# Encoder trunk on one core: residuals go into layer 1's projections and the sample's second SwiGLU without their norm, and the row scale is applied to what comes out

## The chip, the cores and the metric

The kernel runs on one core of a Trainium2 chip. The metric is device microseconds of one execution. Engines are named as in the profile: PE (TensorE, matmuls), DVE (VectorE), ACT (ScalarE), POOL (GpSimd), and SP, which issues nearly all DMAs.

## The reference

Two layers run over a prompt of 1024 tokens and a sample of 512, width 1024, with the same weights. Layer 0 mixes tokens with a Fourier transform, layer 1 with attention; each is followed by a SwiGLU.

```python
def rms_norm(x, g):
    y = xf * lax.rsqrt(jnp.mean(xf * xf, axis=-1, keepdims=True) + EPS)
    return y * g
# layer 1: 8 query heads, 2 key/value heads of 128
h = rms_norm(x, g); q, k, v = split(h @ w_qkv)
q = rope(rms_norm(q, q_gain)); k = rope(rms_norm(k, k_gain))
x = x + softmax(q k^T * 128**-0.5) v @ w_o
# after each layer, inner width 2816
h = rms_norm(x, g)
x = x + (silu(h @ w_gate) * (h @ w_up)) @ w_down
```

The norm's factor is one number a token (a row of x), so it can be taken through a product with weights: `(r*x*g) @ w = r * ((x*g) @ w)`. Queries and keys are normalised once more, head by head.

## The kernel before

Tokens stand in three blocks of 512: block 0 is the sample, 1 and 2 the prompt. A residual is kept transposed, eight tiles of 128 features by 512 tokens. Every fp32 product is made of three matmuls: each operand is split into a rounded part (on ACT, line 242 or 245) and a rest (on DVE or POOL, line 243 or 246), and `mm3` (lines 249 to 251) adds three of the four part products. Three such matmuls are called a triple here.

The code is written as generators, whose `yield` gives an estimated cost; `weave` takes from two of them in turn, the stream F and the stream X, so that their work lies mixed, and a scheduler in the tile framework then sets each engine's order. F and X have PSUM banks and SBUF buffers of their own. The stages: the sample's Fourier mixer; its first SwiGLU with the prompt's mixer (to about 530 us); the prompt's SwiGLU of layer 0 for both blocks at once (`ffn_pair`, to about 1210); then `main_1` in F (the sample's projections, attention, out-projection and second SwiGLU) with `aux_2` in X (the same for the prompt; its reload for the second pair is `moving`); last the prompt's SwiGLU of layer 1, again `ffn_pair`.

- `normed` makes the operand `h` of a projection. From the sums of squares come the factors a token (`rstd`, by `rstd_cols`: four matmuls with a column of ones and a root in small DVE steps); `in_rows` spreads them over the partitions with four matmuls on ones; each of eight residual tiles is multiplied by them on DVE (line 369) into PSUM and split from there (lines 245, 246).
- `normed` is called by `qkv` for the three blocks and by `prepare` for the sample's second SwiGLU. Block 0 is read from DRAM (`xres`), blocks 1 and 2 from SBUF, where `ffn_pair` left them (`kept`).
- `qkv` runs 12 projections of 8 triples. Of each query head the sums of squares go to `ssq`, and one root at the end serves all heads; a key head has a root and rows of its own; a value head is turned on PE and copied out (line 1260).
- `ffn` makes, for each of 22 slices, gate in 8 triples and up in 8, `silu` on ACT (line 851), the product and its split, and the down product into accumulators (line 782). In the sample's first SwiGLU (`here`) it has the row factor applied to gate's and up's sums on DVE (lines 849, 850).
- `attend` takes 128 queries at a time: scores, softmax (`p`), PE transposes of `p` into `pt` (`turned`), and `values` for two such steps.
- `ffn_pair` makes seven products for eight, both for gate and up (tiles `a` of two banks) and for down: `product(k, d, f0)`, 28 for each pair of slices, one triple each, into `chain[d]`, and DVE adds the bank to an accumulator (line 1054). In all pairs of slices but the last the four chains are banks of `bank()` and `bankg()` (tiles `c` and `g`); in the last they are halves of two-bank tiles `a`. Each group of four products reads one operand; the fourth group reads the operand `N4`, kept in the tile `ring`, and it comes from the last gate and up step.

Of the kernel before, what the change touches and what calls it, by code (L numbers as in the profile page):

```python
# [10 lines left out]
F32 = mybir.dt.float32  # L11
# [3 lines left out]
ALU = mybir.AluOpType  # L15
# [110 lines left out]
def trunk_kernel(ctx: ExitStack, tc: tile.TileContext, t: dict):  # L126
# [177 lines left out]
    def rstd_cols(y, sq, n):  # L304

        c = bank()
        for j in range(4):
            pe.matmul(c[:, j : j + 1], sq[:, j * P : (j + 1) * P], ones[:, 0:1], start=True, stop=True)
        rsqrt(y, c[:, 0:4], 1.0 / n, c[:, 8:24])

# [43 lines left out]

    def normed(b, gain, got, ab, held=None):

        settled(b)
        yield 2.0
        r = in_rows(rstd[b])
        h = h_tile(ab)  # L360
        yield 1.0
        for dp in range(NC // 2):
            for dc, ps in zip((2 * dp, 2 * dp + 1), sides()):
                if held is None:
                    x = tmp()
                    sp.dma_start(x, xres[b][:, dc, :])
                else:
                    x = held[dc]
                dve.tensor_tensor(ps, r, x, op=ALU.mult)
                split(h[:, 0, dc], h[:, 1, dc], ps, gain=gain[:, dc : dc + 1])  # L370
            yield 1.5
        got["h"] = h
# [371 lines left out]
    def linear_residual(src, u, b, prev):  # L744

        for n in range(NC):
            w = weights(src[n])
            x = tmp()
            sp.dma_start(x, prev[:, n, :])
            ps = bank()  # L750
            project(w, u, ps)
            dve.tensor_tensor(x, ps, x, op=ALU.add)
            new_residual(b, n, x)
            yield 5.5


    kept, pend = {}, []

    def ffn(layer, b, h, out=None):
        h = h()  # L760
        here = b in resident
        acc = resident.pop(b) if here else accumulators()
# [3 lines left out]
        def halves(ms, wds, f0, dc):  # L766

            box = []

            def half(i):  # L770
                w = wds[dc // 4].rearrange("p h (f c) n -> p h f c n", f=2)
                mm3(box[0], w[:, 0, i, dc % 4], w[:, 1, i, dc % 4], ms[i][:, 0], ms[i][:, 1], i == 0, i == 1)

            def begin():
                box.append(bank())
                if f0 == 0 and not here:
                    sp.dma_start(acc[dc], xres[b][:, dc, :])
                half(0)

            def end():  # L780
                half(1)
                dve.tensor_tensor(acc[dc], box[0], acc[dc], op=ALU.add)  # L782
                if f0 + 2 == NF:
                    new_residual(b, dc, acc[dc], None if out is None else out[:, dc, :])

            return begin, end
# [25 lines left out]
        for fc in range(NF):  # L812
# [19 lines left out]
            for dc in range(NC):  # L832
                if not odd_ and dc == 3:
                    want("gate", fc + 1)
                if fc == NF - 1 and dc == 4:
                    want("B", f0)
                if dc == (2 if odd_ else 4):
                    want("up", fc + 1)
                if not (here and fc == 0):
                    part(wu, h, up, dc)  # L840
                if not odd_:
                    one(2 if dc in (2, 4, 6) else 1)
                elif dc >= 6:
                    one()
                if dc % 2:
                    yield (3.4 if dc > 1 else 2.7) if not odd_ else 2.7 if dc == 7 else 1.36
            s = tmp()
            if here:
                dve.tensor_tensor(ga, ga, first["r"], op=ALU.mult)
                dve.tensor_tensor(up, up, first["r"], op=ALU.mult)  # L850
# [71 lines left out]
    def ffn_pair(layer, blocks, ring, places, outs):  # L922
# [111 lines left out]
        def product(k, d, f0):  # L1034
# [11 lines left out]
            if fresh and f0 + 2 < NF:  # L1046
# [178 lines left out]
    def qkv(b, held=None):  # L1225
        got = {}
        yield from normed(b, g_mix1, got, "ABB"[b], held)
        h = got["h"]
# [13 lines left out]
        def key_sums(j, sq, a):  # L1242

            y = cols.tile([P, 4], F32, tag="yk", name=nm("yk"))
            rstd_cols(y, sq, HD)
# [8 lines left out]
        def turned_values(j, v):  # L1254
# [5 lines left out]
            dve.tensor_copy(vs, vt)  # L1260
            sp.dma_start(dv[b][j - NH - NKV].rearrange("p c n -> p (c n)"), vs)

        def settle():

            now, owed[:] = owed[:], []
            for v in reversed(now):
                v()
# [31 lines left out]
        y = col(4 * NH)  # L1299
        rsqrt(y, ssq.rearrange("p c h -> p (c h)"), 1.0 / HD, bank()[:, 0 : 16 * NH])  # L1300
        dst = slice(4 * b, 4 * b + 4)
# [3 lines left out]
    def attend(blocks, straight, slot):  # L1305
# [6 lines left out]
        for g in range(NKV):  # L1312
# [15 lines left out]
            for h in range(g * GROUP, (g + 1) * GROUP):  # L1328
# [52 lines left out]
                last = None  # L1381
                for qc in range(nk + 1):
                    p = scores(qc) if qc < nk else None
                    yield 0.7 * nb
                    if qc:
                        turned(qc - 1, last)
                        yield 0.8 * nb
                        if qc % 2 == 0:
                            values(qc // 2 - 1)
                            yield 0.8 * nb  # L1390
                    last = p
# [16 lines left out]

    FFN_US, PAIR_US, CHAIN_US, PROMPT_US = 352.0, 678.0, 223.0, 630.0
# [63 lines left out]
    def prepare(b, layer):  # L1473

        yield from normed(b, g_ffn[layer], nxt, "A")
# [65 lines left out]
    def main_1():  # L1541
        yield from qkv(0)
        yield from attend((0,), 0, "A")
        yield from out_projection(0, "A")
# [3 lines left out]
    def aux_2():  # L1548
        for b in (2, 1):
            settled(b)  # L1550
            yield 2.0
# [123 lines left out]
```

## Time and profile before

| | us |
|---|---|
| median of 3 runs (2968.76 to 2973.36) | 2969.23 |
| the profiled execution | 2965.4 |
| its span, first to last instruction | 2963.6 |
| PE busy | 2855.9 |
| DVE busy | 1713.3 |
| POOL busy | 1517.6 |
| ACT busy | 1304.9 |

A row of a group gives line, engine, operation, tiles as out<-in, shapes and the count, then busy time and the mean of one in ns, then the idle time of the engine before it and what ended that. A row of the timeline gives start, length, engine, line and tiles, and in brackets the wait before it with its releaser. A window gives, for PE, weight loads, DVE, ACT and POOL, busy time and number of instructions, then the granted share of PE's clock, the DMA engines' busy share and GB/s. PE's matmuls are pipelined: at full clock, triples of 512 columns start every 0.68 us although each matmul is shown as 0.39 long.

### The profile page before, as it was taken

How to read it: one execution, taken by the hardware profiler on the slowest of the kernel's cores; microseconds unless marked ns; L12 is line 12 of the kernel's file. 1: busy time of each engine (PE TensorE's matmuls, PEld its weight loads, DVE VectorE, ACT ScalarE, POOL GpSimd, SP SyncE). 2: the span in 40 equal slices, each digit the busy share in tenths (PEclk: the TensorE clock that was granted, in tenths of full speed). 3: DMA queues.
4: the chain of work that ended last, by engine and by line, in shares of the span. 5: the costliest groups of instructions: out<-in, count | busy, mean ns of one | idle time of the engine just before them, and what ended most of it. 6: DMA issues, size and time to landing. Idle time of an engine off the chain costs nothing. (4 is left out here: it accounts for less than half of the span.)

```text
span 2963.6 us, 37198 instructions
## 1 busy us (share of the span) xinstructions
PE 2855.9 (96%) x13656; PEld 2350.0 (79%) x13656; DVE 1713.3 (58%) x3031; ACT 1304.9 (44%) x2131; POOL 1517.6 (51%) x932
## 2 busy tenths in 40 slices
PE   7999999999999999998998999999998999999998
PEld 6778878788888887786777888878886788888886
DVE  6674553566666667737646555552244466666666
ACT  5543232333333333646756776663333333333332
POOL 4344264766776774522241122224535767766763
PEclk8999999999999999999999999999999999999999
DMA  7435374766556553632242121115447865565552
GB/s 227 143 116 183 131 270 167 291 218 222 192 186 219 199 175 130 213 93 85 83 150 89 59 91 54 54 57 192 151 168 278 309 235 200 176 219 201 192 195 89
DMA packets 182326, 496.82 MB, mean 168 GB/s; under 512 B 19872, under 2 KB 30112, under 8 KB 180736
## 3 DMA queue, kind: packets, MB, share of 16 engines
q1 hardware_dynamic: 181216, 489.65, 48.5%
q0 software_dynamic: 640, 3.74, 0.4%
q8 instruction: 108, 1.77, 0.2%
q10 hardware_dynamic: 288, 1.05, 0.1%
q14 instruction: 74, 0.61, 0.1%
HBM read 426.21 MB, written 68.16 MB: 167 GB/s over the span
## 5 line engine op out<-in xcount | busy, mean ns | idle before, releaser
L288 POOL TENSOR_TENSOR w<-raw,w 128x1024 fp32r<-128x1024 f32 x200 | 479.0, 2402 | 843.9 <-ACT w L287 832.7
L243 POOL TENSOR_TENSOR w<-raw,w 128x512 fp32r<-128x512 f32 (+1 forms) x464 | 608.3, 1331 | 451.2 <-ACT w L242 445.0
L242 ACT CAST w<-raw 128x512 fp32r<-128x512 f32 (+1 forms) x464 | 279.6, 632 | 538.3 <-PE a L251 173.2
L287 ACT CAST w<-raw 128x1024 fp32r<-128x1024 f32 x200 | 208.7, 1049 | 269.5 <-PE g L251 77.9
L249 PE MATMUL g<-h,w 128*128 128x512 f32 x704 | 279.3, 397 | 9.9 <-ACT w L287 3.4
L251 PE MATMUL g<-h,w 128*128 128x512 f32 x704 | 277.8, 395 | 2.2 <-POOL w L288 2.2
L249 PE MATMUL a<-ring,w 128*128 128x512 f32 x712 | 279.5, 392 | 0.1
L251 PE MATMUL a<-ring,w 128*128 128x512 f32 x712 | 277.5, 390 | 0.0
L250 PE MATMUL a<-ring,w 128*128 128x512 f32 x712 | 277.3, 389 | 0.0
L250 PE MATMUL g<-h,w 128*128 128x512 f32 x704 | 276.8, 393 | 0.0
L1054 DVE TENSOR_TENSOR acc<-g,acc 128x512 f32<-128x512 f32 x280 | 192.5, 687 | 106.9 <-PE g L251 106.6
L1054 DVE TENSOR_TENSOR acc<-c,acc 128x512 f32<-128x512 f32 x280 | 192.4, 687 | 93.7 <-PE c L251 92.1
L249 PE MATMUL c<-mid,w 128*128 128x512 f32 x592 | 232.4, 393 | 13.3 <-ACT mid L242 7.6
L250 PE MATMUL c<-mid,w 128*128 128x512 f32 x592 | 232.6, 393 | 1.2 <-DVE mid L243 1.1
L251 PE MATMUL c<-mid,w 128*128 128x512 f32 x592 | 232.5, 393 | 1.3 <-POOL w L288 1.3
L249 PE MATMUL c<-h,w 128*128 128x512 f32 x480 | 191.5, 400 | 4.3 <-ACT h L245 3.3
L782 DVE TENSOR_TENSOR acc<-c,acc 128x512 f32<-128x512 f32 x176 | 120.9, 688 | 129.2 <-PE c L251 126.5
L250 PE MATMUL c<-h,w 128*128 128x512 f32 x480 | 189.1, 395 | 1.2 <-DVE h L246 0.9
L251 PE MATMUL c<-h,w 128*128 128x512 f32 x480 | 188.9, 394 | 0.0
L249 PEld LDWEIGHTS g<-h,w 128*128 128x128 f32 x704 | 133.0, 189 | 37.1 <-ACT w L287 3.8
L249 PEld LDWEIGHTS a<-ring,w 128*128 128x128 f32 x712 | 133.8, 188 | 33.8 <-DVE mid L243 4.4
L251 PEld LDWEIGHTS g<-h,w 128*128 128x128 f32 x704 | 132.9, 189 | 30.0 <-POOL w L288 3.3
(392 smaller groups left out, 6718.5 us busy)
## 6 DMA issues: line engine op xcount, KB each, us to landing
ring<-mov_B SPq DMA_DIRECT2D x248, 512.0 KB, 5.5
ring<-mov_T SPq DMA_DIRECT2D x88, 512.0 KB, 5.1
raw<-in_gate_dram SPq DMA_DIRECT2D x44, 512.0 KB, 3.6
raw<-in_up_dram SPq DMA_DIRECT2D x44, 512.0 KB, 3.5
raw<-in_down_dram SPq DMA_DIRECT2D x88, 256.0 KB, 3.1
raw<-in_gate_dram SPq DMA_DIRECT2D x88, 256.0 KB, 5.0
raw<-in_up_dram SPq DMA_DIRECT2D x88, 256.0 KB, 5.4
raw<-in_down_dram SPq DMA_DIRECT2D x44, 512.0 KB, 4.1
```

The source lines that it names most:

```text
L242: keep(act.copy(hi, src))
L243: keep(eng.tensor_tensor(lo, src, hi.bitcast(F32), op=ALU.subtract))
L249: pe.matmul(out, lh, rh, start=first, stop=False, **kw)
L250: pe.matmul(out, lh, rl, start=False, stop=False, **kw)
L251: pe.matmul(out, ll, rh, start=False, stop=last, **kw)
L287: pinned(act.copy(flat[:, 0], raw)) if early else act.copy(flat[:, 0], raw)
L288: pool.tensor_tensor(flat[:, 1], raw, flat[:, 0].bitcast(F32), op=ALU.subtract)
L782: dve.tensor_tensor(acc[dc], box[0], acc[dc], op=ALU.add)
L1054: dve.tensor_tensor(acc, chain[d], acc, op=ALU.add)
```

## The change

`normed` is gone. `qkv` and `prepare` split the residual times the gain as it is. In `qkv` the row factor is applied twice to each head's sums of squares and once to the root (`outer`, `by_head`: with sums S of the unscaled head, the factor wanted is r / sqrt(r*r*S/128 + eps)), and to the value copies, which now are four of 128 columns with a factor a partition. The sums of squares of a block are closed (`settled`) at the first head instead of before the operand. In the sample's second SwiGLU the factor is applied to gate's and up's sums, as in the first; its accumulators are taken before the out-projection, which adds into them directly (`staying`), so that the residual is not written to DRAM and read back. Beside this, `ffn_pair` of layer 1 uses the banks `c` and `g` for its last chains too, and the estimated costs in `qkv`, `attend` and `prepare` are others; with `LAG = 1` `attend` issues its steps in the order it had.

```diff
+    def rstd_cols(y, sq, n, outer=None):
...
+        if outer is not None:
+            for _ in range(2):
+                dve.tensor_tensor(c[:, 0:4], c[:, 0:4], outer, op=ALU.mult)
         rsqrt(y, c[:, 0:4], 1.0 / n, c[:, 8:24])
+        if outer is not None:
+            dve.tensor_tensor(y, y, outer, op=ALU.mult)
...
-    def normed(b, gain, got, ab, held=None):
-        settled(b)
-        yield 2.0
-        r = in_rows(rstd[b])
...
-                dve.tensor_tensor(ps, r, x, op=ALU.mult)
-                split(h[:, 0, dc], h[:, 1, dc], ps, gain=gain[:, dc : dc + 1])
...
# linear_residual
-            x = tmp()
+            x = staying[b][n] if b in staying else tmp()
...
-            new_residual(b, n, x)
+            new_residual(b, n, x, stays=b in staying, later=(tl("ss", [TB], F32, "ssF") if n == 0 else ss[b]) if b in staying else None)
...
# ffn
-                if f0 == 0 and not here:
-                    sp.dma_start(acc[dc], xres[b][:, dc, :])
...
+                if fc == 0 and not here and dc == 1:
+                    settled(b)
...
-            if here:
-                dve.tensor_tensor(ga, ga, first["r"], op=ALU.mult)
-                dve.tensor_tensor(up, up, first["r"], op=ALU.mult)
+            if fc == 0 and not here:
+                first["r"] = tl("ss", [TB], F32, "ssF")
+                act.copy(first["r"], in_rows(rstd[b]))
+            dve.tensor_tensor(ga, ga, first["r"], op=ALU.mult)
+            dve.tensor_tensor(up, up, first["r"], op=ALU.mult)
...
# product, in ffn_pair
-            if fresh and f0 + 2 < NF:
+            if fresh and (f0 + 2 < NF or outs is not None):
                 chain[d] = bank() if d % 2 else bankg()
...
# qkv
+        h = h_tile("ABB"[b])
+        yield 0.5
+        for dc in (4, 5, 6, 7, 0, 1, 2, 3):
...
+            split(h[:, 0, dc], h[:, 1, dc], x, gain=g_mix1[:, dc : dc + 1])
+            yield 0.7
...
-            rstd_cols(y, sq, HD)
+            rstd_cols(y, sq, HD, rstd[b])
...
-            dve.tensor_copy(vs, vt)
+            for i in range(4):
+                dve.tensor_scalar(vs[:, i * P : (i + 1) * P], vt[:, i * P : (i + 1) * P], rstd[b][:, i : i + 1], None, op0=ALU.mult)
...
+        by_head = rstd[b].unsqueeze(2).to_broadcast([P, 4, NH])
+        for _ in range(2):
+            dve.tensor_tensor(ssq, ssq, by_head, op=ALU.mult)
...
# attend
+                for qc in range(nk + LAG):
+                    if qc < nk:
+                        ps.append(scores(qc))
+                        yield 0.7 * nb
+                    n = qc - LAG
+                    if n >= 0:
+                        turned(n, ps[n])
+                        yield (0.2 if n % 2 else 2.0) * nb
+                        if n % 2:
+                            values(n // 2)
+                            yield 0.2 * nb
...
# prepare
-        yield from normed(b, g_ffn[layer], nxt, "A")
+        h = h_tile("A")
+        for dc in range(NC):
+            split(h[:, 0, dc], h[:, 1, dc], staying[b][dc], gain=g_ffn[layer][:, dc : dc + 1])
+        nxt["h"] = h
+        yield 1.0
...
# main_1
         yield from attend((0,), 0, "A")
+        staying[0] = accumulators()
         yield from out_projection(0, "A")
...
# aux_2
-        for b in (2, 1):
-            settled(b)
-            yield 2.0
```

What it does to the order is shown at three places. Line numbers of the changed program are its own (its 1366 is 1364 above, 1042 is 1054, 1124 is 1136, 1072 is 1084). First PE at the end of the program, the first four down products of the last pair of slices; before:

```order
L249 MATMUL a_23742<-mid_18667,w_23618 128x512
L250 MATMUL a_23742<-mid_18667,w_23618 128x512
L251 MATMUL a_23742<-mid_18667,w_23618 128x512
L249 MATMUL a_23742<-mid_18667,w_23618 128x512
L250 MATMUL a_23742<-mid_18667,w_23618 128x512
L251 MATMUL a_23742<-mid_18667,w_23618 128x512
L249 MATMUL a_23742<-mid_18669,w_23618 128x512
L250 MATMUL a_23742<-mid_18669,w_23618 128x512
L251 MATMUL a_23742<-mid_18669,w_23618 128x512
L249 MATMUL a_23742<-mid_18669,w_23618 128x512
L250 MATMUL a_23742<-mid_18669,w_23618 128x512
L251 MATMUL a_23742<-mid_18669,w_23618 128x512
```

All four write one tile of two banks. Now, after two products that stand ahead of the last gate step:

```order
L249 MATMUL g_23708<-mid_18637,w_23574 128x512
L250 MATMUL g_23708<-mid_18637,w_23574 128x512
L251 MATMUL g_23708<-mid_18637,w_23574 128x512
L249 MATMUL c_23713<-mid_18637,w_23574 128x512
L250 MATMUL c_23713<-mid_18637,w_23574 128x512
L251 MATMUL c_23713<-mid_18637,w_23574 128x512
L249 MATMUL g_23698<-mid_18639,w_23574 128x512
L250 MATMUL g_23698<-mid_18639,w_23574 128x512
L251 MATMUL g_23698<-mid_18639,w_23574 128x512
L249 MATMUL c_23703<-mid_18639,w_23574 128x512
L250 MATMUL c_23703<-mid_18639,w_23574 128x512
L251 MATMUL c_23703<-mid_18639,w_23574 128x512
```

Each writes a tile of its own, and a tile comes again after four products.

Second PE where the sample's out-projection (`c<-h`) ends, mixed with prompt attention (`a<-w` scores, `c<-ident,p` transposes, `c<-pt` values); before, with the sums of squares (`ss`) behind it:

```order
L249 MATMUL c_13204<-h_10881,w_13199 128x512
L250 MATMUL c_13204<-h_10881,w_13199 128x512
L251 MATMUL c_13204<-h_10881,w_13199 128x512
L249 MATMUL a_13253<-w_12614,w_13178 128x512
L250 MATMUL a_13253<-w_12614,w_13178 128x512
L251 MATMUL a_13253<-w_12614,w_13178 128x512
L249 MATMUL a_13253<-w_12614,w_13178 128x512
L250 MATMUL a_13253<-w_12614,w_13178 128x512
L251 MATMUL a_13253<-w_12614,w_13178 128x512
L1364 MATMUL c_13271<-ident,p_13193 128x128 x4
L1364 MATMUL c_13278<-ident,p_13193 128x128 x4
L308 MATMUL c_13235<-ones,ss_12494 128x1 x4
```

And now, from the transposes that follow the out-projection's last triples:

```order
L1366 MATMUL c_13123<-ident,p_13067 128x128 x4
L1366 MATMUL c_13130<-ident,p_13067 128x128 x4
L251 MATMUL a_13171<-w_12613,w_13168 128x512
L249 MATMUL a_13171<-w_12613,w_13168 128x512
L250 MATMUL a_13171<-w_12613,w_13168 128x512
L251 MATMUL a_13171<-w_12613,w_13168 128x512
L249 MATMUL g_13246<-h_13219,w_13238 128x512
L250 MATMUL g_13246<-h_13219,w_13238 128x512
L251 MATMUL g_13246<-h_13219,w_13238 128x512
L249 MATMUL g_13246<-h_13219,w_13238 128x512
L250 MATMUL g_13246<-h_13219,w_13238 128x512
L251 MATMUL g_13246<-h_13219,w_13238 128x512
```

The first gate triples (`g<-h`) stand directly behind these; before, they came four scores later, behind the sums and the rows.

Third DVE where the sample's projections begin, in the last pair of slices of layer 0 (`a_9352` is the last gate and up step, `a_9392` a tile of down products); before:

```order
L369 TENSOR_TENSOR g_9428<-c_9406,t_9430 128x512
L1054 TENSOR_TENSOR acc_4051<-a_9392,acc_4051 128x512
L1136 TENSOR_TENSOR a_9352<-a_9352,t_4583 128x512
L246 SCALAR_TENSOR_TENSOR h_9419<-g_9428,gains,h_9419 128x512
L1066 TENSOR_TENSOR a_9352<-a_9352,t_4582 128x512
L1054 TENSOR_TENSOR acc_4051<-a_9392,acc_4051 128x512
L1084 TENSOR_TENSOR a_9352<-a_9352,f_4061 128x512
L369 TENSOR_TENSOR g_9429<-c_9406,t_9435 128x512
L1054 TENSOR_TENSOR acc_4053<-a_9392,acc_4053 128x512
```

And now:

```order
L1042 TENSOR_TENSOR acc_4051<-a_9392,acc_4051 128x512
L246 SCALAR_TENSOR_TENSOR h_9397<-t_9398,gains,h_9397 128x512
L1124 TENSOR_TENSOR a_9352<-a_9352,t_4583 128x512
L1042 TENSOR_TENSOR acc_4051<-a_9392,acc_4051 128x512
L1054 TENSOR_TENSOR a_9352<-a_9352,t_4582 128x512
L1072 TENSOR_TENSOR a_9352<-a_9352,f_4061 128x512
L1042 TENSOR_TENSOR acc_4053<-a_9392,acc_4053 128x512
```

The products L369 are gone, and the split reads the reloaded tile `t` instead of PSUM.

More of the change, by code (lines that the diff above doesn't have):

```diff
@@ L302, in rsqrt @@
             keep(dve.scalar_tensor_tensor(z if k < 2 else y, a, 1.5, z, op0=ALU.add, op1=ALU.mult))
-    def rstd_cols(y, sq, n):
+    def rstd_cols(y, sq, n, outer=None):
         c = bank()
@@ L353, in settled @@
             rstd_cols(rstd[b], ss.pop(b), D)
-    def normed(b, gain, got, ab, held=None):
-        settled(b)
-        yield 2.0
-        r = in_rows(rstd[b])
[L360 to L364, printed above, removed]
-                    x = tmp()
[L366 to L369, printed above, removed]
-                split(h[:, 0, dc], h[:, 1, dc], ps, gain=gain[:, dc : dc + 1])
-            yield 1.5
-        got["h"] = h
     def reloaded(d, got, ab):
@@ L747, in linear_residual @@
             w = weights(src[n])
-            x = tmp()
+            x = staying[b][n] if b in staying else tmp()
             sp.dma_start(x, prev[:, n, :])
@@ L752, in linear_residual @@
             dve.tensor_tensor(x, ps, x, op=ALU.add)
-            new_residual(b, n, x)
+            new_residual(b, n, x, stays=b in staying, later=(tl("ss", [TB], F32, "ssF") if n == 0 else ss[b]) if b in staying else None)
             yield 5.5
-    kept, pend = {}, []
+    kept, pend, staying = {}, [], {}
     def ffn(layer, b, h, out=None):
@@ L761, in ffn @@
         here = b in resident
-        acc = resident.pop(b) if here else accumulators()
+        acc = resident.pop(b) if here else staying[b]
         kept[b] = acc
@@ L1225, in qkv @@
     def qkv(b, held=None):
-        got = {}
-        yield from normed(b, g_mix1, got, "ABB"[b], held)
-        h = got["h"]
+        h = h_tile("ABB"[b])
+        yield 0.5
+        for dc in (4, 5, 6, 7, 0, 1, 2, 3):
+            if held is None:
+                x = tmp()
+                sp.dma_start(x, xres[b][:, dc, :])
+            else:
+                x = held[dc]
+            split(h[:, 0, dc], h[:, 1, dc], x, gain=g_mix1[:, dc : dc + 1])
+            yield 0.7
         rope = tl("rope", [2, TB], F32, "pX", ap) if cur[0] == "X" else tl("rope", [2, TB], F32, "mid")
@@ L1265, in settle @@
             now, owed[:] = owed[:], []
+            settled(b)
             for v in reversed(now):
@@ L1299, in qkv @@
         y = col(4 * NH)
+        by_head = rstd[b].unsqueeze(2).to_broadcast([P, 4, NH])
+        for _ in range(2):
+            dve.tensor_tensor(ssq, ssq, by_head, op=ALU.mult)
         rsqrt(y, ssq.rearrange("p c h -> p (c h)"), 1.0 / HD, bank()[:, 0 : 16 * NH])
+        yv = y.rearrange("p (c h) -> p c h", c=4)
+        dve.tensor_tensor(yv, yv, by_head, op=ALU.mult)
         dst = slice(4 * b, 4 * b + 4)
@@ L1379, in values @@
                     sp.dma_start(dot[blocks[n]][:, h, c0 : c0 + 256], o)
[L1381 to L1391, printed above, removed]
+                ps = []
+                for qc in range(nk + LAG):
[9 more added lines that the diff above has]
+                            yield 0.2 * nb
     def weave(main, main_cost, aux=None, aux_cost=1.0, lead=0):
@@ L1407, in weave @@
         cur[0] = "F"
+    LAG = 1
     FFN_US, PAIR_US, CHAIN_US, PROMPT_US = 352.0, 678.0, 223.0, 630.0
```

## Prediction

> **What bounds the kernel now.** I read the page first (busy shares, chain), then the windows by stage, then PE's rows in the two stages where it idles most.
>
> ```profile
> PE 2855.9 (96%) x13656; PEld 2350.0 (79%) x13656; DVE 1713.3 (58%) x3031; ACT 1304.9 (44%) x2131; POOL 1517.6 (51%) x932
> PE 42%; DVE 2%; ACT 1%; POOL 1%; DMA 1%; issue 1%; SPq 0%; POOLq 0%; ACTq 0%; DVEq 0%
> L288 POOL TENSOR_TENSOR w<-raw,w 128x1024 fp32r<-128x1024 f32 x200 | 479.0, 2402 | 843.9 <-ACT w L287 832.7
> ```
>
> PE is the bound: 2855.9 of 2963.6 us, and 42% of the chain against 2% for DVE. All that can be won is PE's missing 108 us, its half-clock stretches, and matmuls that go. Where these lie:
>
> ```profile
> core 0: us, PE busy (x) PEld busy (x) DVE busy (x) ACT busy (x) POOL busy (x), PEclk, DMA share, GB/s
> 250.00:300.00 50.00, 50.00 (x304) 44.75 (x303) 27.19 (x67) 15.71 (x20) 21.97 (x10) 1.00 0.57 180
> 1150.00:1215.00 65.00, 58.06 (x252) 42.66 (x250) 58.56 (x88) 36.36 (x58) 25.39 (x16) 1.00 0.50 168
> 1215.00:1300.00 85.00, 83.50 (x412) 68.43 (x412) 40.83 (x89) 45.00 (x65) 38.07 (x16) 1.00 0.48 156
> 1300.00:1400.00 100.00, 91.68 (x471) 72.69 (x469) 61.60 (x171) 58.97 (x112) 21.09 (x12) 1.00 0.24 77
> 1602.00:1637.00 35.00, 25.36 (x137) 21.62 (x136) 25.40 (x58) 22.75 (x38) 2.35 (x1) 0.85 0.22 68
> 1637.00:2000.00 363.00, 351.03 (x2006) 296.44 (x2005) 200.65 (x367) 252.18 (x353) 89.63 (x38) 1.00 0.19 64
> 2195.00:2335.00 140.00, 127.81 (x533) 102.66 (x532) 60.14 (x91) 47.67 (x74) 84.18 (x49) 0.95 0.80 282
> 2905.00:2964.00 59.00, 49.24 (x184) 33.84 (x182) 37.66 (x57) 12.47 (x22) 17.70 (x14) 0.93 0.19 72
> ```
>
> The first number behind the stage's length is PE's busy time. In order of time the stages are: the sample's first SwiGLU (250:300), the end of the prompt's first pair with the sample's projections (1150:1215), the two prompt blocks' projections, the gap between the sample's out-projection and its second SwiGLU (1602:1637), prompt attention, the prompt's reload for the second pair (2195:2335), and the end. Idle PE: 6.9, 1.5, 8.3, 9.6, 12.0, 12.2 and 9.8 us from 1150 on, with half clock besides at 1602 (mean 0.85) and in the last stage (0.93).
>
> **The end of the program (the edit of `fresh`).**
>
> The rows are the timeline's for PE and DVE; the last one is a window.
>
> ```profile
> 2928.25 0.39 PE L249 MATMUL a<-late,w 128*128 128x512 f32 x1
> 2929.11 0.50 PE L249 MATMUL a<-mid,w 128*128 128x512 f32 x1
> 2930.86 0.51 PE L249 MATMUL a<-mid,w 128*128 128x512 f32 x1 [0.79 <-DVE acc L1054]
> 2932.87 0.47 PE L249 MATMUL a<-mid,w 128*128 128x512 f32 x1 [1.04 <-DVE acc L1054]
> 2941.88 0.47 PE L249 MATMUL a<-ring,w 128*128 128x512 f32 x1
> 2959.19 0.40 PE L251 MATMUL a<-mid,w 128*128 128x512 f32 x1
> 2930.11 0.69 DVE L1054 TENSOR_TENSOR acc<-a,acc 128x512 f32<-128x512 f32 x1 [0.28 <-PE a L251]
> 2930.72 0.69 DVE L1136 TENSOR_TENSOR a<-a,t 128x512 f32<-128x512 f32 x1
> 2936.39 0.68 DVE L243 TENSOR_TENSOR ring<-a,ring 128x512 fp32r<-128x512 f32 x1
> 2936.00:2942.00 6.00, 5.38 (x13) 4.07 (x14) 3.15 (x5) 0.00 (x0) 0.00 (x0) 0.50 0.00 0
> ```
>
> After the last gate matmul 28 down products follow, three matmuls each, from 2929.11 to 2959.19: 30.1 us. At the free pitch of 0.68 us a product (2928.25 is the start of such a triple; 1600.78 to 1601.46 below is another) they would take 19. The reason stands in the brackets: two products share a two-bank tile `a`, so the second waits until DVE has added the first, although it writes the other bank. Now each of four products has a bank of its own and is met again four products later, 2.7 us against an addition of 0.69. The new order also puts two products ahead of the last gate step and leaves 26. What is late next is `N4`: the fourth group of products reads `ring`, ready at 2937.1, 8.0 us after 2929.1. Ten products (6.8 us) stand before it now, and DVE does four more additions on the way, each 0.61 (2930.11 to 2930.72), so `ring` comes after 8.0 to 10.4 us; then 16 products, 10.9 us. Together 21.3 at the later value against 30.1: **-8.8**. Ends: -11.2 if `ring` keeps its 8.0; -5.5 if the clock halves for 6 us again, as at 2936:2942, which costs 3 us more. [...]
>
> **The gap before the sample's second SwiGLU (unnormalised `h`).**
>
> ```profile
> 1600.78 0.39 PE L249 MATMUL c<-h,w 128*128 128x512 f32 x1
> 1601.46 0.39 PE L249 MATMUL a<-w,w 128*128 128x512 f32 x1
> 1607.13 0.57 PE L249 MATMUL a<-w,w 128*128 128x512 f32 x1 [1.71 <-ACT p L1350]
> 1620.62 0.50 PE L249 MATMUL a<-w,w 128*128 128x512 f32 x1 [1.93 <-ACT p L1350]
> 1627.21 0.50 PE L249 MATMUL a<-w,w 128*128 128x512 f32 x1 [2.45 <-ACT p L1350]
> 1636.19 0.50 PE L249 MATMUL g<-h,w 128*128 128x512 f32 x1 [2.10 <-DVE h L246]
> ```
>
> The last out-projection triple starts at 1600.78, the first gate triple at 1636.19. Between them stand squares, sums, the root, rows, eight reloads, eight products, eight splits; prompt attention alone feeds PE and its own softmax shows (`ACT p L1350`). Now the splits read the residual kept in SBUF, and the first gate triple stands behind one score and one turn of attention, about where the out-projection ends. Price: 137 matmul records in 35 us; at the pace of the next stage, 2006 in 363, they would take 24.8: **-10** (10.2). Ends: 0, if attention elsewhere gives up the cover that it gets here, and -16, if idle time (9.6) and half clock (the missing 0.15 of 35, 5, and some) both go.
>
> **The three blocks' projections.**
>
> ```profile
> L369 DVE TENSOR_TENSOR a<-c,acc 128x512 f32<-128x512 f32 x16 | 11.1, 694 | 0.2
> L369 DVE TENSOR_TENSOR g<-c,t 128x512 f32<-128x512 f32 x16 | 10.7, 691 | 0.5 <-DMA t<-xres 0.3 <-PE c L317 0.2
> L246 DVE SCALAR_TENSOR_TENSOR h<-g,gains,h 128x512 fp32r<-128x512 f32 x16 | 11.5, 744 | 1.0 <-ACT h L245 1.0
> L246 DVE SCALAR_TENSOR_TENSOR h<-acc,gains,h 128x512 fp32r<-128x512 f32 x8 | 6.5, 834 | 1.5 <-ACT h L245 1.5
> L339 DVE TENSOR_TENSOR ss<-sq,ss 128x512 f32<-128x512 f32 x14 | 14.8, 1061 | 0.1
> L849 DVE TENSOR_TENSOR g<-g,ss 128x512 f32<-128x512 f32 x22 | 15.3, 696 | 21.9 <-PE g L251 21.8
> L1240 DVE COPY ssq<-c 128x4 f32<-128x4 f32 x24 | 4.0, 166 | 38.5 <-PE c L1239 38.5
> L1260 DVE COPY t<-c 128x512 f32<-128x512 f32 x6 | 4.1, 687 | 6.9 <-PE c L1258 6.8
> L851 ACT ACT_TABLE_LOAD x12 | 15.4, 1283 | 0.2
> ```
>
> All 32 products L369 go (21.8 us of DVE), and 12 row matmuls. At 1150:1215 DVE is busy 58.6 of 65, so 8 x 0.69 would be worth 5.5; but the order now has five products in a row on one tile `a`, with four waits of 0.8 to 1.0 each and no projection matmul between them. I take **-1** (ends -5 and +4). In 1215:1300 PE idles only 1.5: **-1**. In 1300:1400 it idles 8.3, DVE loses eight products and the root from the path of block 1's first projection; half of that idle time: **-4** (ends -8 and +2).
>
> **What is added.** 44 products in the SwiGLU, 0.696 each: 30.6 us of DVE in 1637 to 2330 (busy 200.65 of 363 in prompt attention, 60.14 of 140 in the reload). Gate's runs under up's eight triples (5.4 us), up's delays the next operand by 0.7; the first SwiGLU has both products, and at 250:300 PE is busy 50.00 of 50. In prompt attention they queue before the softmax: **+1.5** (ends 0 and 30.6). Head norms and value copies: 27 small products and 24 quarter copies for 6 whole ones. At L1240's 0.17 they take 8.7, less 4.1; with quarter copies as long as whole ones (L1260, 0.69) 17: 5 to 17 us of DVE, the small end nearer, on chains that end under the next projection's 24 matmuls: **+0.5** (ends 0 and 3). Two more table loads, 1.28 each, on ACT at 252 of 363: **+0.5** (ends 0 and 2.6). Gone: 24 transfers issued by SP, the eight reloads and eight accumulator loads before the second SwiGLU among them; SP has no row in the chain, so 0 (the cover is prompt attention; without it they ended in the gap already counted). Yields in attention and projections move what lies between scores, turns and values; counted in the order at full pitch, sample work inside prompt attention is 198 us of matmul time against 194: 0. At 2195:2335 the reload moves by a few triples against the SwiGLU, 92 triples of gate and up left behind the last sums for 97: 0 (ends -4 and +4).
>
> **Sum.** -8.8 - 10 - 1 - 1 - 4 + 1.5 + 0.5 + 0.5 = -22.3 us. The profiled execution took 2965.4 (span 2963.6), so it would take 2943; the median of the three runs, 2969.2, lies 3.8 above it, and on its scale the forecast is **2947 us**.
>
> **Rivals.**
> 1. *The gap's cover is borrowed.* The 10 us come back, as sample matmuls used at 1602 lack under later softmax steps: 12.3 us are left, 2957. For it: the sum of cover in attention is nearly unchanged (198 for 194). Against: before, single steps there had 3 to 4 us of cover while steps at 1610 to 1630 had under 1; now nearly every pair has 2.7.
> 2. *Splits held up by POOL.* L339 with both inputs in SBUF averages 1.061, and L246 from `acc` 0.834 against 0.744 from PSUM. All 32 splits now have both inputs in SBUF. A split that meets a POOL instruction of 2.4 us waits half of it, 1.2, and POOL is busy 0.4 of 1150:1300: 0.5 each; 16 of them lie in the stage where DVE is the bound: +8, 2955. Against: L246's own 0.834, which makes it 1.4. [...]
> 3. *The products of the SwiGLU reach PE (slower than before).* In prompt attention waits for `p` and `pt` end on ACT and DVE; if each of 44 products lengthens such a chain by its whole 0.696, 30.6 come in place of 1.5: +6.8, 2976. It decides from 24 us on, 0.54 a product. Against: 200.65 of 363 on DVE, and 250:300.
>
> **How the numbers follow.** Forecast 0.60 (own range 2937 to 2956: bounds of the end, of the gap and of the projections, which hardly all fall on one side), the first rival 0.20, the second 0.10, the third 0.04; 0.06 for more than the forecast's range, when `ring` comes early and the half clock goes everywhere. From 2934 to 2961 leaves out the third rival and about half of the tails. 0.2% is 6 us, about what a measurement of this kernel can tell from no change: below 2963 lie the forecast, the surplus and all but a quarter of the first two rivals: faster 0.88; same 0.08; slower 0.04.
>
> **What would show it.** The last group of products takes 20 to 24 us from the last `late` matmul to the last matmul, on tiles `g` and `c`, with at most one wait of 1 to 4 us before `ring`. The first `g<-h` of the second SwiGLU starts within 6 us of the last out-projection triple, and PE's mean clock there is 1.00. PE's idle time at 1150 to 1215 stays at 5 to 9 us; DVE is 20 to 30 us busier between 1640 and 2330 with PE as busy as now. The forecast is wrong if PE's idle share in prompt attention rises from 3% to 6%, if L246 averages over 1.1 us, or if the reload stage grows by more than 5 us.

## The result and the profile after

The changed kernel took 2950.8 us, median of four runs (2947.3 to 2953.1), beside 2969.0 of the kernel before (four runs, 2966.2 to 2973.4): ratio 0.9936, 95% interval 0.9919 to 0.9954. The forecast was 2947, range 2934 to 2961. The profiled execution has a span of 2950.5 us and took 2952.3.

From the page of the changed kernel, the busy times and the chain by engine:

```profile
PE 2847.3 (97%) x13632; PEld 2348.3 (80%) x13632; DVE 1736.4 (59%) x3088; ACT 1305.0 (44%) x2122; POOL 1516.0 (51%) x932
PE 39%; issue 2%; DVE 2%; POOL 2%; DMA 1%; ACT 1%; SPq 0%; POOLq 0%; ACTq 0%; DVEq 0%
```

PE is still the bound; its busy time fell by 8.6 us and its idle time by 4.5. The stages of the prediction again, in the windows of the changed kernel:

```profile
core 0: us, PE busy (x) PEld busy (x) DVE busy (x) ACT busy (x) POOL busy (x), PEclk, DMA share, GB/s
1150.00:1215.00 65.00, 55.38 (x217) 40.47 (x216) 51.24 (x72) 35.67 (x58) 22.37 (x14) 0.89 0.43 144
1215.00:1300.00 85.00, 80.55 (x392) 67.36 (x392) 40.49 (x75) 42.47 (x58) 41.65 (x18) 0.98 0.57 182
1602.00:1637.00 35.00, 33.64 (x193) 27.76 (x191) 26.52 (x57) 26.99 (x43) 7.37 (x3) 1.00 0.16 49
1637.00:2000.00 363.00, 352.33 (x2028) 298.48 (x2029) 216.75 (x398) 260.20 (x366) 89.71 (x38) 1.00 0.18 58
2195.00:2335.00 140.00, 124.57 (x518) 99.33 (x517) 63.70 (x96) 44.47 (x69) 82.98 (x50) 0.95 0.81 284
```

Two things stand out: the gap at 1602 has filled (193 matmuls in 35 us for 137, clock 1.00 for 0.85), and the stage at 1150 has become worse (217 matmuls for 252, clock 0.89 for 1.00).

Runs of one kernel within one experiment spread by up to 15 us, part of it ahead of the change. On PE the programs are the same up to 1155 us, and but for four small row matmuls up to the last `late` matmul of the first pair; among the fourteen profiles of this study, before, after and experiments, that matmul starts anywhere from 1158.6 to 1167.7 us. So the profiles are compared from there to the last matmul; this stretch is called the rest of the program below. In the timeline of PE, the kernel before:

```profile
1162.09 0.40 PE L251 MATMUL a<-late,w 128*128 128x512 f32 x1
```

Its last matmul starts at 2959.19: the rest is 1797.1 us. In the changed kernel it goes from 1162.01 to 2944.91, 1782.9 us, and 1780.4 in a second profile. By stages, each from the start of one matmul to that of another:

| stage | before | after | after, second profile |
|---|---|---|---|
| last `late` to the sample's first score (`g<-w`) | 185.4 | 192.3 | 191.2 |
| to the sample's last out-projection matmul (`c<-h`) | 253.8 | 250.4 | 248.3 |
| to prompt attention's last score (`a<-w`) | 393.6 | 389.9 | 391.2 |
| to the second SwiGLU's last up matmul (`g<-h`) | 306.5 | 303.7 | 303.4 |
| to the last `late` matmul of the second pair | 627.3 | 626.9 | 626.7 |
| to the last matmul | 30.5 | 19.7 | 19.6 |
| sum | 1797.1 | 1782.9 | 1780.4 |

The end and the gap did as forecast. PE's rows at the end (start, duration, engine, line, tiles), and those around the gap:

```profile
2925.26 0.39 PE L251 MATMUL a<-late,w 128*128 128x512 f32 x1
2925.48 0.39 PE L249 MATMUL g<-mid,w 128*128 128x512 f32 x1
...
2933.80 0.40 PE L249 MATMUL g<-ring,w 128*128 128x512 f32 x1
...
2944.91 0.39 PE L251 MATMUL c<-mid,w 128*128 128x512 f32 x1
```

```profile
1604.75 0.39 PE L251 MATMUL c<-h,w 128*128 128x512 f32 x1
1605.85 0.50 PE L249 MATMUL a<-w,w 128*128 128x512 f32 x1 [0.71 <-ACT p L1352]
...
1609.10 0.40 PE L249 MATMUL g<-h,w 128*128 128x512 f32 x1
```

The last group of products runs on `g` and `c` at nearly the free pitch: 26 products in 19.7 us, where 17.7 would be free. PE comes to `ring` 8.3 us after the first product, with the eleventh, and hardly waits for it. The second SwiGLU starts 4.4 us behind the out-projection in place of 35.

The loss is at 1162. First the kernel before, its first projection matmul; then the changed kernel, PE's rows (each triple by its first matmul, those without a wait left out in part), and DVE's and POOL's beside them:

```profile
1165.56 0.51 PE L249 MATMUL c<-h,w 128*128 128x512 f32 x1 [0.71 <-ACT h L245]
```

```profile
1162.42 0.50 PE L249 MATMUL a<-mid,w 128*128 128x512 f32 x1
...
1164.18 0.50 PE L249 MATMUL a<-mid,w 128*128 128x512 f32 x1 [0.78 <-DVE acc L1042]
...
1167.92 0.77 PE L249 MATMUL a<-mid,w 128*128 128x512 f32 x1 [2.77 <-DVE acc L1042]
1168.48 0.63 PE L250 MATMUL a<-mid,w 128*128 128x512 f32 x1
...
1170.32 0.79 PE L249 MATMUL a<-mid,w 128*128 128x512 f32 x1 [0.78 <-DVE acc L1042]
...
1172.84 0.76 PE L249 MATMUL a<-mid,w 128*128 128x512 f32 x1 [0.88 <-DVE acc L1042]
...
1176.53 0.80 PE L249 MATMUL a<-mid,w 128*128 128x512 f32 x1 [0.78 <-DVE acc L1042]
...
1180.30 0.40 PE L249 MATMUL c<-h,w 128*128 128x512 f32 x1
...
1163.65 2.37 POOL L288 TENSOR_TENSOR w<-raw,w 128x1024 fp32r<-128x1024 f32 x1
1164.19 2.38 DVE L246 SCALAR_TENSOR_TENSOR h<-t,gains,h 128x512 fp32r<-128x512 f32 x1
1167.10 0.68 DVE L1042 TENSOR_TENSOR acc<-a,acc 128x512 f32<-128x512 f32 x1
```

Nine products stand in a row on two-bank tiles `a`; five of them wait for DVE, 6.0 us together. The longest wait holds the addition behind a split of 2.38 us, which began 0.54 us into a POOL instruction. From 1168 on matmuls stand 0.43 us apart in place of 0.23: the clock is half from 1166.4 to 1180.0, and the 21 matmuls of seven products take some 4 us more (an estimate, 21 times 0.2). The window's clock is the number behind POOL's:

```profile
1166.50:1180.00 13.50, 9.64 (x20) 6.10 (x21) 10.22 (x17) 4.51 (x8) 0.00 (x0) 0.50 0.53 164
```

The first projection matmul comes at 1180.30, 18.3 us after the last `late` matmul; before, it came 3.5 us after. This is no accident of one run: the changed kernel's second profile and those of five experiments that keep the row have half clock of the same length there (mean 0.83 from 1155 to 1195 in all seven); the kernel before has none, and the same code with the new end 3.4 us (mean 0.96).

### The profile page after: what moved, and what is told of

It reads as the page before. It is cut to its first block, busy times and chain, and to the rows that moved or that the text cites. A ratio compares the mean times of both kernels' runs of the same rounds, so it can differ in the third digit from the quotient of the medians.

```text
span 2950.5 us, 37155 instructions
## 1 busy us (share of the span) xinstructions
PE 2847.3 (97%) x13632; PEld 2348.3 (80%) x13632; DVE 1736.4 (59%) x3088; ACT 1305.0 (44%) x2122; POOL 1516.0 (51%) x932
## 5 line engine op out<-in xcount | busy, mean ns | idle before, releaser
L1042 DVE TENSOR_TENSOR acc<-g,acc 128x512 f32<-128x512 f32 x294 | 201.8, 686 | 105.3 <-PE g L251 104.9
L1042 DVE TENSOR_TENSOR acc<-c,acc 128x512 f32<-128x512 f32 x294 | 201.7, 686 | 92.6 <-PE c L251 90.9
L249 PE MATMUL c<-mid,w 128*128 128x512 f32 x604 | 238.4, 395 | 14.5 <-ACT mid L242 10.2
L250 PE MATMUL c<-mid,w 128*128 128x512 f32 x604 | 238.1, 394 | 1.1 <-DVE mid L243 1.1
L251 PE MATMUL c<-mid,w 128*128 128x512 f32 x604 | 237.2, 393 | 0.7 <-POOL w L288 0.7
L766 DVE TENSOR_TENSOR acc<-c,acc 128x512 f32<-128x512 f32 x176 | 120.7, 688 | 116.2 <-PE c L251 115.5
```

Of the source, the lines that this page charges most:

```text
L249: pe.matmul(out, lh, rh, start=first, stop=False, **kw)
L250: pe.matmul(out, lh, rl, start=False, stop=False, **kw)
L251: pe.matmul(out, ll, rh, start=False, stop=last, **kw)
L1042: dve.tensor_tensor(acc, chain[d], acc, op=ALU.add)
```

## The experiments

Each experiment is told by its median over five rounds, its ratio to the kernel before with the 95% interval, and the rest of the program in its profile; the last leaves out what varies ahead of the change, but is of one profile each, and the changed kernel's is put at 1781.7, the mean of its two.

### The end alone

```diff
 # the kernel before, with
-if fresh and f0 + 2 < NF:
+if fresh and (f0 + 2 < NF or outs is not None):
```

> The kernel before with the edit of `fresh` alone. Theory (the end is worth what the two profiles show there, 30.5 us against 19.65 from the last `late` matmul to the last matmul): 10.8 us less than before, 2958 us, and the last stretch on tiles g and c as in the changed kernel. Rival (the end got shorter because other parts of the change left fewer products or other work there): under 5 us less, 2964 us or more, with the last stretch above 25 us.

Measured: 2961.5 us, ratio 0.998 (0.997 to 0.9991); rest 1786.2, 10.9 less than before. The last `late` matmul and the last matmul:

```profile
2933.87 0.39 PE L251 MATMUL a<-late,w 128*128 128x512 f32 x1
...
2953.54 0.39 PE L251 MATMUL c<-mid,w 128*128 128x512 f32 x1
```

19.7 us, as in the changed kernel, so the gain at the end is this edit's. The median fell by 4.0 only, with an interval of 3 to 9 us, which leaves out the 10.9. This profile reached the last `late` matmul of the first pair 5.2 us later than that of before, in code that is the same; whether that is chance isn't shown. The next experiment has 8.6 for this stretch where no half clock strikes, which lies inside the interval.

### The end taken back

```diff
 # the changed kernel, with
-if fresh and (f0 + 2 < NF or outs is not None):
+if fresh and f0 + 2 < NF:
```

> The changed kernel without the edit of `fresh`. Theory (the end is worth 10.9 us whatever comes before it, as the kernel before with this edit alone had it in its profile): the last stretch from the last `late` matmul takes 30 to 31 us again, and the whole 10 to 11 us more, 2961 to 2963 us beside 2951.9. Rival (part of it is given back, as the whole time of the kernel before fell by only 4.0 us with this edit alone): 4 to 6 us more, 2956 to 2958 us.

Measured: 2957.9 us, ratio 0.996 (0.9945 to 0.9974); rest 1789.1, 7.5 more than the changed kernel.

```profile
2928.59 0.39 PE L251 MATMUL a<-late,w 128*128 128x512 f32 x1
...
2956.85 0.40 PE L251 MATMUL a<-mid,w 128*128 128x512 f32 x1
```

```profile
2936.00:2942.00 6.00, 5.34 (x20) 3.44 (x21) 4.67 (x8) 0.00 (x0) 0.00 (x0) 1.00 0.00 0
```

The old end takes 28.3 us here, 30.5 in the profile of before: the first two rows are of the timeline, the third is the window in which the kernel before had its half clock (0.50), and here it is 1.00. So this stretch gets 8.6 us shorter, and 2.2 more where the half clock strikes. Two products (1.4 us) now stand ahead of it, so the end is worth some 7 to 9.5 us, an estimate; the rest of the program has 7.5 and 10.9. The expected 30 to 31 us and 2961 us were too much; the rival's 2956 to 2958 holds for the median, but nothing is given back later, since nothing comes later.

### The sample's second SwiGLU as before

```diff
 # the changed kernel, with
-        for dc in range(NC):
-            split(h[:, 0, dc], h[:, 1, dc], staying[b][dc], gain=...)
+        yield from normed(b, g_ffn[layer], nxt, "A")
 # and the accumulators loaded late, no products on ga and up
```

> The changed kernel, but the sample's second SwiGLU takes a normalised residual again: eight reloads, eight products, splits from PSUM, accumulators loaded late, no products on gate's and up's sums. Theory (the gap of 1602 to 1637 us is worth 8 to 10 us net of what the products cost): 8 to 10 us more than the changed kernel, 2959 to 2961 us, with PE busy under 27 of 35 us in the gap. Rival (the gap's cover is borrowed): 0 to 3 us more, 2951 to 2954 us, with prompt attention's idle time smaller by as much as the gap's is larger.

Measured: 2960.3 us, ratio 0.998 (0.9967 to 0.9993); rest 1792.5, 10.8 more. Its windows at the gap and in prompt attention:

```profile
1602.00:1637.00 35.00, 26.52 (x145) 21.69 (x144) 28.36 (x61) 25.21 (x42) 4.78 (x2) 0.92 0.27 87
1637.00:2000.00 363.00, 351.76 (x2026) 297.82 (x2025) 203.57 (x374) 256.54 (x360) 86.01 (x36) 1.00 0.19 62
```

The gap is back, and attention's busy time is that of the changed kernel (351.8 and 352.3): the cover was not borrowed. The gap, less what the products cost, is worth 10.8 us.

### The sample's projections as before

```diff
 # the changed kernel; for b == 0 in qkv
-        for dc in (4, 5, 6, 7, 0, 1, 2, 3): ... split(..., x, ...)
+        yield from normed(0, g_mix1, got, "A")
 # and no outer factor in sums, roots and value copies of block 0
```

> The changed kernel, but the sample's projections (block 0) take a normalised residual again: row products into g, splits from PSUM, no outer factor, whole value copies. Theory (the change lost 7 to 10 us of PE time between 1150 and 1300 us, because layer 1's projections on block 0 start behind a row of products on one tile a): 7 to 9 us less than the changed kernel, 2942 to 2944 us, first c<-h before 1167 us. Rival (the loss there comes out of cover that later stages use anyway, so it is only moved): within 2 us of the changed kernel, 2949 to 2953 us.

Measured: 2957.1 us, ratio 0.997 (0.9959 to 0.9981); rest 1785.8, 4.1 more than the changed kernel: neither theory. The first `c<-h` came 3.1 us behind the last `late` matmul, as expected, but the loss stood 45 to 60 us later. PE's two longest waits there, and DVE and POOL at the first of them:

```profile
1214.01 0.80 PE L249 MATMUL a<-mid,w 128*128 128x512 f32 x1 [3.62 <-DVE acc L1061]
1228.60 0.76 PE L249 MATMUL c<-h,w 128*128 128x512 f32 x1 [4.47 <-DVE ssq L1262]
...
1206.44 5.17 POOL L288 TENSOR_TENSOR w<-raw,w 128x1024 fp32r<-128x1024 f32 x2 [9.11 <-ACT w L287]
...
1207.23 2.17 DVE L246 SCALAR_TENSOR_TENSOR h<-acc,gains,h 128x512 fp32r<-128x512 f32 x1
1209.33 2.83 DVE L344 TENSOR_TENSOR ss<-sq,ss 128x512 f32<-128x512 f32 x1
```

Now block 2's split, in the new form, meets POOL's two instructions, and the next DVE instruction with both inputs in SBUF the second of them. Taking back block 0's arithmetic left these and reordered what follows; it didn't isolate the loss.

### The splits in natural order

```diff
 # the changed kernel, for all three blocks, with
-        for dc in (4, 5, 6, 7, 0, 1, 2, 3):
+        for dc in range(NC):
```

> The changed kernel with one thing different: the splits of the three projections run over pieces 0 to 7 in natural order in place of 4 to 7 first. The projections' matmuls read piece 0 first, so in the changed kernel the first c<-h stands behind nine products (27 matmuls) on tile a, and here behind one. Theory (the missing matmuls between the products cost 5 to 7 us at 1162 to 1181 us): first c<-h within 5 us of the last `late` matmul, no half clock there, 4 to 7 us less than the changed kernel. Rival (splits with both inputs in SBUF are what costs): the 2.4 us split stays and with it most of the loss, 0 to 2 us less.

Measured: 2945.6 us, ratio 0.9924 (0.991 to 0.9939); rest 1773.1, 8.6 less than the changed kernel. In the timeline of PE, and of DVE (last row):

```profile
1165.56 0.39 PE L251 MATMUL a<-late,w 128*128 128x512 f32 x1
1165.97 0.50 PE L249 MATMUL a<-mid,w 128*128 128x512 f32 x1
...
1167.81 0.50 PE L249 MATMUL c<-h,w 128*128 128x512 f32 x1 [0.88 <-ACT h L245]
...
1170.19 0.80 PE L250 MATMUL c<-h,w 128*128 128x512 f32 x1 [1.19 <-DVE h L246]
...
1173.82 0.80 PE L249 MATMUL a<-mid,w 128*128 128x512 f32 x1 [0.78 <-DVE acc L1042]
...
1167.79 2.35 DVE L246 SCALAR_TENSOR_TENSOR h<-t,gains,h 128x512 fp32r<-128x512 f32 x1
```

One product, then the first projection matmul. The slow split is still there, and so is some half clock (10 us from 1170 on, in place of 14); yet the loss is gone, 6.0 of the 8.6 us ahead of the sample's first score. The gain is the theory's or more (8.6 by the rest, 6.2 between the medians of this kernel and the changed one in the same rounds, for 4 to 7 us), but its "no half clock" doesn't hold. The kernel before had the natural order, so this order is a part of the change.

### Block 0's splits from PSUM

```diff
 # the changed kernel; pieces that are loaded again
-                x = tmp()
-                sp.dma_start(x, xres[b][:, dc, :])
+                t_ = tmp()
+                sp.dma_start(t_, xres[b][:, dc, :])
+                x = side()
+                act.copy(x, t_)
```

> The changed kernel with one more step for block 0: each reloaded piece is copied to a PSUM tile g by ACT, and the split reads that, so that no split there has both inputs in SBUF. Theory (a split of 2.38 us at 1164.2 us beside a POOL instruction starts the loss): the wait of 2.77 us before PE at 1168 and the half clock after it go, 4 to 6 us less than the changed kernel, 2945 to 2947 us, and no split L246 there above 0.9 us. Rival (the row of five products on one tile a is what waits, with or without a slow split): the waits of 0.8 to 0.9 us and the half clock stay, within 2 us of the changed kernel.

Measured: 2947.7 us, ratio 0.9939 (0.9924 to 0.9953); rest 1776.9, 4.8 less than the changed kernel. The first split, POOL's instruction beside it, PE's longest wait behind it, and the group of all eight splits (the two numbers behind the first bar: busy us, mean ns):

```profile
1166.55 0.74 DVE L246 SCALAR_TENSOR_TENSOR h<-g,gains,h 128x512 fp32r<-128x512 f32 x1
1165.02 2.37 POOL L288 TENSOR_TENSOR w<-raw,w 128x1024 fp32r<-128x1024 f32 x1
1168.63 0.77 PE L249 MATMUL a<-mid,w 128*128 128x512 f32 x1 [2.15 <-DVE acc L1042]
```

```profile
L246 DVE SCALAR_TENSOR_TENSOR h<-g,gains,h 128x512 fp32r<-128x512 f32 x8 | 5.9, 743 | 0.4 <-ACT h L245 0.4
```

0.74 beside POOL's weight split of 2.37, where the same split from SBUF took 2.38. The gain is as expected, but the mechanism is not: a wait of 2.15 us for `acc` stayed, with three DVE instructions of 0.7 us ahead of the addition in place of the long split, and half clock stayed for 10 us in place of 14.

### All splits from PSUM

```diff
 # as above, for kept blocks too
+            x = side()
+            act.copy(x, held[dc])
```

> The changed kernel with ACT copies of the pieces to PSUM ahead of the splits, as in the run with block 0's alone, now for all three blocks' projections (24 copies of 0.59 us on ACT). Theory (splits with both inputs in SBUF wait for POOL): no split L246 of the projections above 0.9 us, and the waits on the sums `ssq` of 1.7 and 1.8 us at 1216 to 1226 us get shorter: 1 to 3 us less than with block 0's alone, 6 to 9 us less than the changed kernel. Rival (ACT, busy half of that time, becomes what the projections wait for): 0 to 4 us more than with block 0's alone.

Measured: 2951.1 us, ratio 0.9945 (0.9932 to 0.9957); rest 1781.4: 4.5 more than with block 0's alone, just over the rival's 0 to 4, though single profiles hardly tell such a difference. It is not by ACT as the rival had it. DVE's row, POOL's beside it, and PE's wait:

```profile
1219.46 2.71 DVE L344 TENSOR_TENSOR ss<-sq,ss 128x512 f32<-128x512 f32 x1
...
1219.29 2.34 POOL L288 TENSOR_TENSOR w<-raw,w 128x1024 fp32r<-128x1024 f32 x1 [3.35 <-ACT w L287]
...
1222.30 0.79 PE L249 MATMUL c<-h,w 128*128 128x512 f32 x1 [3.38 <-DVE ssq L1237]
```

No split from PSUM takes more than 0.75 us; the sums `ss<-sq,ss`, which read SBUF twice, meet POOL in their place.

### Natural order, and block 0 from PSUM

```diff
 # the two edits above together, the copies for block 0 alone
-        for dc in (4, 5, 6, 7, 0, 1, 2, 3):
+        for dc in range(NC):
```

> The changed kernel with the splits in natural order and, for block 0, read from a PSUM copy. The natural order alone stands at 1773.1 us from the last `late` matmul of the first pair to the last matmul, against 1782.9 and 1780.4 for the changed kernel. Theory (order and slow splits cost each by itself): the 2.35 us split at 1168 goes too, 2 to 4 us less than with the order alone, 1769 to 1771 us. Rival (once projection matmuls stand between the products, DVE's delay of 1.6 us is covered): within 1.5 us of the order alone, or more by what ACT's copies cost.

Measured: 2943.3 us beside 2968.7, ratio 0.9909 (0.9895 to 0.9924); rest 1773.0, the same as with the order alone: the rival. The last `ring` matmul of the first pair comes 4.6 us earlier than with the order alone, and the clock is 1.00 from 1164 to 1180, but a wait for `ssq` behind block 2's splits gives it back before the sample's first score:

```profile
1227.13 0.80 PE L249 MATMUL c<-h,w 128*128 128x512 f32 x1 [3.80 <-DVE ssq L1237]
```

By its ratio this is the fastest version run, and it beats the changed kernel run in the same manner (0.9949, 0.9936 to 0.9962) and the kernel before; by the rest of the program it and the order alone are equal, both 8.6 us below the changed kernel.

### The products of the second SwiGLU

```diff
 # the changed kernel, for the sample's second SwiGLU
-            dve.tensor_tensor(ga, ga, first["r"], op=ALU.mult)
-            dve.tensor_tensor(up, up, first["r"], op=ALU.mult)
```

> The changed kernel without the 44 products of the row scale on gate's and up's sums in the sample's second SwiGLU; the output lacks that scale. Theory (they lie beside PE, except in prompt attention): 0 to 3 us less than the changed kernel. Rival (each lengthens a chain that PE waits for): 20 us less or more, at least 0.5 us a product.

Measured: 2946.1 us, ratio 0.9924 (0.9909 to 0.9939); rest 1772.5, 9.2 less. Between theory and rival. 5.4 of it lie after prompt attention, up to the SwiGLU's last matmul. With up's 22 left out alone:

```diff
-            dve.tensor_tensor(up, up, first["r"], op=ALU.mult)
```

> The changed kernel without the 22 products of the row scale on up's sums in the sample's second SwiGLU (gate's 22 stay); the output lacks that scale on up. Without all 44 the stretch from the last `late` matmul of the first pair to the last matmul was 1772.5 us, against 1782.9 and 1780.4 for the changed kernel: 9.2 us, 0.21 a product. Theory (gate's products run under up's matmuls, up's stand between up's last matmul and the next operand `mid`): leaving out up's alone wins 6 to 9 us of the 9.2, 1773 to 1776 us. Rival (what costs is DVE's time, whichever product takes it): half, 4 to 5 us, 1777 to 1778 us. Third: the 9.2 comes from the pace of the reload stage at 2195 to 2335 us (5.4 of it lay there) and is not in proportion to the products: 0 to 3 us, 1779 to 1782 us.

Measured: 2952.0 us, ratio 0.9946 (0.9932 to 0.996); rest 1783.9, nothing won, the third theory. The reload stage, without all 44 and without up's:

```profile
2195.00:2335.00 140.00, 129.08 (x539) 103.53 (x538) 58.84 (x89) 46.11 (x73) 88.09 (x53) 0.95 0.83 297
```

```profile
2195.00:2335.00 140.00, 124.39 (x512) 98.83 (x511) 58.33 (x87) 43.70 (x68) 81.92 (x50) 0.95 0.80 280
```

DVE is as little busy in both, PE is not. The kernel without all 44 has its instructions in another order as well (319 of PE's 13632 rows stand elsewhere, and 34 of SP's transfers), the one without up's hardly (24 rows, no transfer). So 22 products cost nothing, and whether the other 22 or the order made the 9 us stays open.

### Attention's steps as before

```diff
-                        yield (0.2 if n % 2 else 2.0) * nb
+                        yield 0.8 * nb   # and 0.8 behind a value product
```

> The changed kernel with the loop of attention as before (a step of 0.7, 0.8 and 0.8 a block in place of 0.7 and then 2.0 or 0.2). Theory (the steps only move the same cover about, as the forecast had it): within 2 us of the changed kernel, 1780 to 1784 us from the last `late` matmul of the first pair to the last matmul. Rival (a value product right behind its turn is what the changed steps avoid): 4 us more or more, with PE's waits for `p` and `pt` from 1637 to 2000 us grown by as much.

Measured: 2950.6 us, ratio 0.9938 (0.9923 to 0.9952); rest 1783.8, 2.1 more. The steps moved matmuls about and won 2 us at most.

### The changed kernel again

> The changed kernel itself, to stand beside the three others. From the last `late` matmul of the first pair (up to where the program is the same as before) to the last matmul its first profile has 1782.9 us, the kernel before 1797.1. If that stretch repeats within 2 us, the spread of whole times comes from elsewhere; if it varies by 5 us or more, differences of that size between single profiles mean nothing. Whole time 0.992 to 0.995 of the kernel before.

Measured: 2951.9 us (2946.6 to 2955.2), ratio 0.9949 (0.9936 to 0.9962); rest 1780.4 beside 1782.9. So differences of 3 us between single profiles of the rest say nothing, and the 4 to 5 us of three kernels above say little without the rows that were shown with them. Two profiles are few: that differences of 7 us and more are real rests on the medians, which went the same way each time.

## Why the prediction was right, and the step that failed

The time is 3.8 us above the forecast, inside the range: two of the three terms below came near the forecast, and the range of 27 us had room for the third, which came out with the wrong sign. Term by term, on the rest of the program:

| term | forecast | measured |
|---|---|---|
| end | -8.8 | -8.6 to -10.9 |
| gap, with the 44 products | -8.5 | -10.8 |
| everything else: projections, head norms, table loads, steps, reload | -5.0 | +4 to +6 |
| sum | -22.3 | -14.2 and -16.7 |

The last measured term is what the other two leave of the mean, -15.4, so their errors are in it.

*The end.* The step was right in its mechanism: separate banks, and 19.7 us forecast as 21.3. Its parts were off and made up for one another. The ten products ahead of `ring` took 8.3 us and not 6.8, as some waited for DVE's additions (0.32 and 0.17 us); `ring` was complete at 8.7 and not 10.4, so the wait of 3.6 us, 10.4 less 6.8, didn't come; and the 1.4 us of the two products put ahead have no term in the forecast. That the close is good is partly luck. Half a clock for 6 us, 3 us more, makes the smaller end -5.8, not -5.5. The half clock in the kernel before, which the forecast counted in its 30.1, doesn't belong to that code: the same products ran at 1.00 from 2936 to 2942 in the changed kernel with the old end.

*The gap.* Right in mechanism and size: 193 matmuls for 137, clock 1.00, `g<-h` within 6 us. The first rival is excluded by the kernel with the old SwiGLU, where PE is no busier in prompt attention.

*The products.* "+1.5 (ends 0 and 30.6)": open between 0 and 9. In prompt attention they cost PE nothing that can be seen (352.3 busy for 351.0, DVE 16 us busier); the third rival, 30.6, is excluded, since leaving out all 44 won 9.2 at most.

*The projections.* This is the step that failed: "the order now has five products in a row on one tile `a`, with four waits of 0.8 to 1.0 each ... I take -1 (ends -5 and +4)". The stage up to the sample's first score became 6.9 and 5.8 us longer, and PE's idle time at 1150 to 1215 went to 9.6 us, outside the forecast's own sign of 5 to 9. The row was seen, and four waits came as read (0.8 to 0.9); but nine products stand in it, not five, and two things had no term. A row without other matmuls has nothing to cover a late DVE: a fifth wait came, 2.77 us, behind the slow split. And the clock fell to half for 13.7 us, which nearly doubled the pitch of seven products. That the natural order of splits takes 8.6 us off again shows where the row comes from: the projections read piece 0 first, and in the changed order it is the fifth to be split. That order stood in the diff, and the forecast gave it no price of its own. The slow split is not what the row needs to be late: without it, a wait of 2.15 us stood at the same product. What the -4 of 1300 to 1400 came to was not measured by itself.

*Splits held up by POOL.* The second rival was partly there. All 40 splits with a gain of the changed kernel, by group (count, then min, median and max ns, then first and last start):

```profile
L246 DVE SCALAR_TENSOR_TENSOR h<-acc,gains,h x32: 725/743/2881, 75.3 to 1615.7; 128x512 fp32r<-128x512 f32 x32
L246 DVE SCALAR_TENSOR_TENSOR h<-t,gains,h x8: 742/745/2385, 1164.2 to 1184.5; 128x512 fp32r<-128x512 f32 x8
```

The median is untouched; five splits of 1.26 to 2.88 us lie from 1164 to 1372 and lose 6.2 us of DVE together, 0.26 for each of the projections' 24 splits in place of the rival's 0.5; their medians hide them. Taking block 0's away went with 4.8 us less while they fell on an uncovered row, and with no gain in the rest of the program once the row was broken up. The delay beside POOL is in the rows: POOL's weight split ran from 1163.65 for 2.37 us, and DVE's split from 1164.19 ended 0.55 us behind it, while the one that read PSUM took 0.74 beside the same POOL instruction.

## What to carry to other kernels

When a producer's order is changed, look up what the consumer reads first: a chain that starts with the fifth piece leaves its neighbours uncovered, and one permutation was worth about half of what the whole change won (8.6 beside 15.4 us). Price an uncovered row of dependent matmuls by all that can stand on DVE ahead of its release, one long instruction or three short ones, not by the mean of one. And compare profiles from the last instruction that the programs have in common, since what lies ahead of it varied by 9 us here.

## What the runs showed of the hardware

In three places half clock was granted at waits of 2.77 us and less. In the changed kernel it was 0.50 from 1166.4 on, behind a wait of 0.78 us and 1.3 us into that of 2.77. With block 0's splits from PSUM it came at the wait of 2.15: the matmul behind that is shown 0.77 us long, and the mean clock from 1150 to 1215 is 0.92; in the changed kernel a matmul behind a wait is shown 0.50 long at full clock (at 1164.18) and 0.76 to 0.80 at half clock (from 1167.92 to 1176.53). In the kernel before 0.50 was granted from 2935.2 on, behind waits of 0.79, 1.04 and 0.78. The old end had 0.50 from 2936 to 2942 there and 1.00 in the changed kernel with that end; what decides it was not shown. And the delay of DVE beside POOL moved on: with all splits from PSUM, two of the sums `ss<-sq,ss`, which read SBUF twice, took 2.86 and 2.71 us in place of 0.68, beside weight splits of 2.39 and 2.34 on POOL.
